# Moving keys ahead of queries, and odd weight pairs into attention's buffers, in a two-layer hybrid decoder trunk

## Chip, cores and metric

The kernel runs on one core of one Trainium2 chip. The metric is device time in microseconds. A core has five engines that work at once, each through its own instructions in order: TensorE (PE, with its weight loads as PEld), VectorE (DVE), ScalarE (ACT), GpSimd (POOL) and SyncE (SP, which here only issues DMAs). Matmuls write PSUM banks; DVE and ACT empty them.

## The reference

Two decoder layers over 512 tokens of width 1024, float32. Each layer normalizes x, projects it, runs two token mixers side by side, adds their gated sum, and then an MLP:

```python
h = rmsnorm(x, norm_mix)
proj = h @ w_in                      # q, k, v of FoX; q, and six k/v of NSA; gates
o_a = fox_attention(...)             # 8 heads, causal softmax with a learned decay
kc, vc = compress_blocks(kc), compress_blocks(vc)      # 31 block summaries
o_c, o_s, o_w = nsa_attention(q_n, kc, vc, ks, vs, kw, vw)   # 8 heads, 2 key/value heads
o_n = g[..., 0:1] * o_c + g[..., 1:2] * o_s + g[..., 2:3] * o_w
mixed = sigmoid(gate_a) * y_a + sigmoid(gate_b) * y_b
x = x + mixed @ w_out
h = rmsnorm(x, norm_mlp)
x = x + square(relu(h @ w_up)) @ w_down                # 1024 -> 4096 -> 1024
```

With 512 tokens the selected branch (s) takes all 8 blocks and the window branch (w) all tokens, so both are plain causal attention with keys ks and kw.

## The kernel before, in words

**Precision and weights.** Every float32 operand is split into a high and a low part (`uh`/`ul`, `wh`/`wl`), and a product is three matmuls: high x high, high x low, low x high (`gemm`, L236 to L238). A weight block is fetched on SP into a raw buffer (`fetch`, L194; tag `raw` has 2 buffers), split by ACT (L210) and DVE (L211), and used. `order` writes out by hand in which order all blocks of both layers are fetched; from the seventh block of the down weights on, they go to one buffer of tag `crs`.

**Who orders the instructions.** The program is written for a framework that gives each instruction the place of its program line as priority, allots buffers by tag as they come free, and orders each engine's queue ahead of the run by a model of the durations. An instruction that is ready early may be placed ahead of earlier lines that are not; on the chip each queue then runs in that order.

**Attention.** `attend` takes units (one head and branch) through three steps: scores, transposes of the softmax, values. Between the steps it draws from a filler generator: 1.8 filler steps per round in FoX, 0.95 in NSA. A projection (`proj`) is 24 matmuls in four filler steps. FoX's filler `fill1` projects the later FoX heads, kc and vc, then runs `compress` in turns with a chain of projections; it ends with the window key kw (block 11 of `wb`). `k_pair` and `q_pair` split the projected rows (ACT, DVE L377) and lay them out for both heads with four DMAs each on SP (L388 into `kk`, L401 into `q`). NSA's filler `fill2` holds `cmp_gen` (`cmp_probs`: the compressed branch of one key/value head, first matmul at L723, which needs two query pairs), `qproj(2)`, `qproj(3)`, and `gated(m)`: two gate projections (DVE multiplies by R at L992), then two output halves. A unit of NSA pair 0 needs query pair 0, ks and kw; its scores are L555 and L558, reduced by DVE at L545. The gate projections and output halves take turns in the two PSUM banks of tag `mm`.

**MLP.** The first 8 of 32 up blocks are plain products. The other 24 make 12 pairs (g = 4 to 15), each a seven-product Strassen scheme (`Strassen.unit`, matmuls at L1382). For a pair, `load` fetches two raw blocks on SP (L1339), adds one half onto another by an accumulating DMA from POOL (L1344, `raw<-raw`), and `third` makes one more sum the same way (L1350 and L1351). `convert` forms two sums on DVE (L1367, L1368) and splits all seven operands (ACT L1371, DVE L1372). Even pairs' raws lie in tag `e` (attention's softmax), odd pairs' in tag `raw`, thirds in `t2`. While pair g is multiplied, pair g + 1 is converted and pair g + 2 loaded. Between the products run down products, whose sums DVE adds to x (L1085), which frees their banks. The activations' sums t3 and t4 lie in tag `va` (4 buffers), which before that held FoX's values and then the mixer's sums MA.

**Constants.** `setup` loads masks and tables (`ct`, L773) and clears `CC`, `kcz` and `vz` on POOL (L781), each with a buffer of its own; the norm's row R lies in tag `r` (L318).

Of the kernel before, what the change touches and what calls it, by code (L numbers as in the profile page):

```python
# [11 lines left out]
F32 = mybir.dt.float32  # L12
# [7 lines left out]
T = 512  # L20
# [123 lines left out]
class Body:  # L144
    def __init__(self, ctx, tc, nc, a):
# [6 lines left out]

    BUFS = dict(raw=2, wh=2, wl=2, uh=8, ul=8, oh=8, ol=8, va=4, t2=12, kd=2, kk=1, zz=4, pt=10, e0=1, ct=1, CC=1, vz=1, q2=3, vn=1, e=2, tmp=3,
                hl=2, r=1, crs=1, small=1, cc=1, s4=6, big=1, kcz=1, g4=2)

# [127 lines left out]

    def rstd(self, acc, tags=("O", "O"), wait=iter(()), exp=True, copy=True):
# [32 lines left out]
        R = self.t("r", [128, T], name="R")[:, :128 * n]  # L317
        nc.scalar.copy(R, ps)  # L318
        return R, rc

# [59 lines left out]
    def k_pair(self, x, fox=None, kd=None):  # L380


        hl = self.hilo(x, 1.0)
        if kd is None:
            kd = self.t("kd", [128, 2, 2, T], F32R)
        for e in range(2):
            for f in range(2):
                self.nc.sync.dma_start(kd[f * 64:(f + 1) * 64, e].bitcast(F32),  # L388
                                         hl[e * 64:(e + 1) * 64].bitcast(F32))
            if fox is not None:  # L390
                h = 2 * fox + e
                self.nc.sync.dma_start(kd[64:66, e, 1].bitcast(F32), self.CC[h:h + 33:32].bitcast(F32))
        return kd
# [22 lines left out]
    def scores(self, u):  # L416
        nc = self.nc
        q, k = u["q"](), u["k"]()
        E = self.t("e", [128, 1280], name="E")
        sm = self.t("s4", [128, NB], name="sm")  # L420
# [111 lines left out]
    def pair_scores(self, u):  # L532
# [3 lines left out]
        q, kk, br, e, other = u["q"](), u["kk"](), u["br"], u["e"], u["other"]  # L536
        E = self.t("e", [128, 1280], name="E")
        if br == 0:
# [10 lines left out]
        for i in range(br, NB):  # L549
            n = 128 * (i + 1)  # L550
            ps = self.p("S")
            qs = q[:, i * 128:(i + 1) * 128]
            for f in range(2):
                if i == 0:
                    nc.tensor.matmul(ps[:, :256].rearrange("p (b c) -> p b c", b=2), qs, kk[:, :, u["hk"], f, :128],  # L555
                                     start=f == 0, stop=f == 1)
                else:
                    nc.tensor.matmul(ps[:, :n], qs, kk[:, br, u["hk"], f, :n], start=f == 0, stop=f == 1)  # L558
# [207 lines left out]
    def setup(self, first):  # L766

        nc, a = self.nc, self.a
        if first:
            self.ident = self.cp.tile([128, 128], F32, name="ident")  # L770
            nc.sync.dma_start(self.ident, a["const"][:, :128])
        self.ct = self.t("ct", [128, 1024])[:, :N_CONST - 128]
        nc.sync.dma_start(self.ct, a["const"][:, 128:])  # L773
        if first:
            self.load_small(0)
        self.mask = self.const("mask")
        self.CC = self.t("CC", [40, T], F32R)
        self.kcz = self.t("kcz", [128, 2, 2, 256], F32R)[:, :, :, :224]
        self.vz = self.t("vz", [128, 2, 2, 128], F32R)
        for t in (self.CC, self.kcz, self.vz):  # L780
            nc.gpsimd.memset(t.bitcast(F32), 0.0)  # L781
# [40 lines left out]
    def order(self, l):  # L822
# [27 lines left out]
    def layer(self, l, u):  # L850
# [8 lines left out]
        for _ in range(6 if l else 8):  # L859
            next(g)  # L860
        self.R, self.rc = R, rc = self.rstd(self.acc, ("O", "O"), wait=g)
        run(g)
# [44 lines left out]
        def fox_unit(h):  # L907
            p, e = divmod(h, 2)
            un = dict(q=lambda: st["qa", p][0][:, e], qx=lambda: st["qa", p][1][e], k=lambda: st["ka", p][:, e], O=[None],
                      ready=lambda: ("qa", p) in st and ("ka", p) in st,  # L910
# [22 lines left out]
        def fill1():  # L933
# [10 lines left out]
        KK = self.t("kk", [128, 2, 2, 2, T], F32R)  # L944
        run(fox_proj(0, ("PT", "PT")))
        self.attend([fox_unit(h) for h in range(8)], fill1(), self.FOX_FILL)


# [3 lines left out]
        def nsa_pair(p):  # L952
# [20 lines left out]
            def unit(br, e):  # L973
                return dict(br=br, e=e, p=p, hk=hk, O=O, after=after, ready=ready[br], kk=lambda: KK,
                            q=lambda: st["qb", p][:, e], v=lambda b: VN[:, b, 2 * br + hk],
# [29 lines left out]
        def fill2():  # L1005
# [58 lines left out]
    def mlp(self, l, x, u, acc, gm):  # L1064
# [50 lines left out]
        for i in range(12):  # L1115
# [149 lines left out]
class Strassen:  # L1265
# [65 lines left out]

    def load(self, g):

        if g < 16:
            b = self.b
            self.raw[g] = []
            for m in (2 * g + 1, 2 * g):
                t = b.t(("e", "raw")[g % 2], [128, 1024], name="raw")
                self.nc.sync.dma_start(t, b.a["wup"][self.l, m].rearrange("p k c -> p (k c)"))  # L1339
                self.raw[g].append(t)  # L1340
            r1, r2 = self.raw[g]
            if g > b.PLAIN // 2:
                self.raw[g].append(self.third(g))
            self.nc.gpsimd.dma_start(r2[:, :512], r2[:, 512:], accum_op=OP.add)  # L1344

    def third(self, g):

        b = self.b
        s3 = b.t("t2", [128, 512], name="s")
        self.nc.sync.dma_start(s3, b.a["wup"][self.l, 2 * g].rearrange("p k c -> p (k c)")[:, :512])  # L1350
        self.nc.gpsimd.dma_start(s3, self.raw[g][0][:, :512], accum_op=OP.add)  # L1351
        return s3

    def convert(self, g):
# [3 lines left out]
        b, nc = self.b, self.nc  # L1358
        if len(self.raw[g]) == 2:
            self.raw[g].append(self.third(g))  # L1360
        r1, r2, s3 = self.raw.pop(g)
# [126 lines left out]
```

## Time and profile before

| what | value |
|---|---|
| median of 3 runs | 1540.74 us (1539.62 to 1543.52) |
| the profiled execution's own time | 1540.51 us |
| its span, first to last instruction | 1538.7 us |
| mean granted TensorE clock | 0.996 |
| busy: PE, DVE, ACT, POOL | 98%, 72%, 53%, 12% |
| moved by DMA | 188.82 MB, 123 GB/s in the mean |

In a profile row, `out<-in` names the tiles written and read, `xN` counts instructions, and a bracket `[1.78 <-DVE gate L992]` gives the engine's idle time before the instruction in us and what ended it. In a view of waits the numbers are the total, the times and the longest. Layer 0 runs from 0 to about 756 us, layer 1 from there on.

### The profile page before, as it was taken

What the parts mean: (1) busy time and instruction counts of PE and PEld (TensorE: products, weight loads), DVE (VectorE), ACT (ScalarE), POOL (GpSimd) and SP (SyncE); (2) the same over time, 40 slices, a digit from 0 to 9 for tenths busy, and PEclk for the clock granted to TensorE, in tenths of its full rate; (3) what the DMA queues carried; (4) which work ended last, traced back from release to release, by engine and by line L of the source; (5) the groups of instructions that cost most, each with busy time, mean ns of one, the idle gap of its engine ahead of it and who ended that gap; (6) DMA issues with size and microseconds to landing.
All of it is one profiled execution on the core that took longest, in us unless ns stands there. A gap on an engine that the chain in (4) does not pass through costs nothing.

```text
span 1538.7 us, 21231 instructions
## 1 busy us (share of the span) xinstructions
PE 1514.2 (98%) x7696; PEld 1264.6 (82%) x7696; DVE 1102.5 (72%) x2124; ACT 811.0 (53%) x1530; POOL 190.1 (12%) x184
## 2 busy tenths in 40 slices
PE   9999999999999999999999999999999999999997
PEld 8878787888888878888888787888888878788897
DVE  5678888777477877775647798877674968777762
ACT  6465555654454655555445555555544636555553
POOL 4000000000201222111310000000002002222122
PEclk9999999999999999999999999999999999999998
DMA  7655322224226555432546542222423365554221
GB/s 261 166 141 150 109 83 84 68 90 162 97 96 177 144 146 140 137 89 87 177 134 179 145 130 83 84 81 69 156 84 97 102 183 135 148 139 136 83 83 55
DMA packets 67576, 188.82 MB, mean 123 GB/s; under 512 B 8560, under 2 KB 9968, under 8 KB 67472
## 3 DMA queue, kind: packets, MB, share of 16 engines
q1 hardware_dynamic: 56672, 168.31, 35.2%
q0 software_dynamic: 6912, 12.59, 5.0%
q10 hardware_dynamic: 3888, 6.58, 1.2%
q8 instruction: 60, 0.98, 0.3%
q14 instruction: 44, 0.36, 0.1%
HBM read 147.53 MB, written 4.19 MB: 99 GB/s over the span
## 4 chain that ended last, share of the span: by engine, by line
PE 83%; DVE 9%; ACT 4%; DMA 3%; issue 2%; SPq 0%; POOL 0%; DVEq 0%; ACTq 0%; POOLq 0%
PE ps_mm L236 11%; PE ps_mm L237 11%; PE ps_mm L238 11%; PE ps_PT L236 3%; PE ps_PT L237 3%; PE ps_PT L238 3%; PE ps_O L1382 3%; PE ps_S L1382 3%; PE ps_mm L1382 2%; PE ps_S L236 2%; PE ps_S L237 2%; PE ps_S L238 2%; PE ps_O L609 2%; PE ps_PT L583 2%; PE ps_O L237 2%; PE ps_O L236 2%
## 5 line engine op out<-in xcount | busy, mean ns | idle before, releaser
L210 ACT CAST wh<-raw 128x1024 fp32r<-128x1024 f32 (+2 forms) x187 | 192.3, 1028 | 261.5 <-issue 81.1
L211 DVE TENSOR_TENSOR wl<-raw,wh 128x1024 fp32r<-128x1024 f32 (+2 forms) x187 | 224.8, 1202 | 48.6 <-ACT wh L210 43.6
L236 PE MATMUL ps_mm<-uh,wh 128*128 128x512 f32 x512 | 204.5, 399 | 0.0
L238 PE MATMUL ps_mm<-uh,wl 128*128 128x512 f32 x512 | 201.8, 394 | 0.0
L237 PE MATMUL ps_mm<-ul,wh 128*128 128x512 f32 x512 | 201.6, 394 | 0.0
L236 PE MATMUL ps_mm<-oh,wh 128*128 128x512 f32 (+1 forms) x316 | 123.4, 392 | 4.0 <-DVE gate L992 3.6
L237 PE MATMUL ps_mm<-ol,wh 128*128 128x512 f32 (+1 forms) x316 | 122.8, 389 | 0.0
L238 PE MATMUL ps_mm<-oh,wl 128*128 128x512 f32 (+1 forms) x316 | 122.6, 388 | 0.0
L238 PEld LDWEIGHTS ps_mm<-uh,wl 128*128 128x128 f32 x512 | 96.4, 188 | 20.8 <-issue 0.8
L236 PEld LDWEIGHTS ps_mm<-uh,wh 128*128 128x128 f32 x512 | 96.4, 188 | 19.3 <-DVE wl L211 1.5
L237 PEld LDWEIGHTS ps_mm<-ul,wh 128*128 128x128 f32 x512 | 96.5, 189 | 16.3
L587 ACT CAST pth<-ps_PT 128x384 fp32r<-128x384 f32 (+1 forms) x96 | 49.1, 513 | 59.0 <-PE ps_PT L583 58.4
L545 DVE CUSTOM_DVE_ANT_0 E<-ps_S,ct 128x384 f32<-128x384 f32 (+3 forms) x112 | 57.1, 514 | 31.1 <-PE ps_S L558 26.8
L1372 DVE TENSOR_TENSOR sl<-raw,sh 128x512 fp32r<-128x512 f32 x96 | 72.7, 760 | 7.2 <-ACT sh L1371 6.4
L546 ACT ACTIVATE E<-E,tiny 128x384 f32<-128x384 f32 (+3 forms) x112 | 65.5, 586 | 21.5 <-DVE tiny L545 21.2
L1371 ACT CAST sh<-raw 128x512 fp32r<-128x512 f32 x96 | 59.1, 617 | 29.4 <-PE ps_mm L1382 10.5
L236 PEld LDWEIGHTS ps_mm<-oh,wh 128*128 128x128 f32 x316 | 59.7, 189 | 17.9 <-DVE gate L992 5.0
L588 DVE TENSOR_TENSOR ptl<-ps_PT,pth 128x384 fp32r<-128x384 f32 (+1 forms) x96 | 57.1, 600 | 18.0 <-ACT pth L587 16.9
L238 PEld LDWEIGHTS ps_mm<-oh,wl 128*128 128x128 f32 x316 | 59.8, 189 | 12.3
L236 PE MATMUL ps_PT<-oh,wh 128*128 128x512 f32 x172 | 67.7, 394 | 2.1 <-DVE x L1085 2.1
L1344 POOL DMA_DIRECT2D raw<-raw x24 | 21.3, 889 | 389.0 <-PE ps_O L609 352.2
L237 PEld LDWEIGHTS ps_mm<-ol,wh 128*128 128x128 f32 x316 | 59.9, 190 | 10.8 <-DVE ol L500 0.4
(444 smaller groups left out, 3989.0 us busy)
## 6 DMA issues: line engine op xcount, KB each, us to landing
raw<-wb SPq DMA_DIRECT2D x64, 512.0 KB, 3.7
raw<-wup SPq DMA_DIRECT2D x64, 512.0 KB, 3.5
raw<-wd SPq DMA_DIRECT2D x48, 512.0 KB, 3.4
w<-w SPq DMA_DIRECT2D x32, 256.0 KB, 4.6
kd<-hl SPq DMA_DIRECT2D x32, 256.0 KB, 5.3
q<-hl SPq DMA_DIRECT2D x64, 128.0 KB, 3.0
raw<-wo SPq DMA_DIRECT2D x16, 512.0 KB, 4.1
raw<-wout SPq DMA_DIRECT2D x16, 512.0 KB, 3.4
```

Of the source, the lines that this page charges most:

```text
L210: nc.scalar.copy(h[:, :n], raw[:, :n])
L211: nc.vector.tensor_tensor(lo[:, :n], raw[:, :n], h[:, :n].bitcast(F32), op=OP.subtract)
L236: mm(ps, h[:, c], xh, start=start and i == 0, stop=False)
L237: mm(ps, h[:, c], xl, start=False, stop=False)
L238: mm(ps, lo[:, c], xh, start=False, stop=stop and i == ks - 1)
L545: nc.vector.tensor_tensor_reduce(e, ps, self.mask[:, T - n:], -1.0, BIG, OP.add, OP.min, mx)
L546: nc.scalar.activation(e, e, AF.Exp, bias=mx, scale=-1.0, accum_out=un["sm"][:, i:i + 1])
L587: nc.scalar.copy(h[:, e, :n], ps[:, :n])
L588: nc.vector.tensor_sub(lo[:, e, :n], ps[:, :n], h[:, e, :n].bitcast(F32))
L1371: nc.scalar.copy(h, src)
L1372: nc.vector.tensor_tensor(lo, src, h.bitcast(F32), op=OP.subtract)
L1382: mm = lambda o, w, x, **kw: self.nc.tensor.matmul(o, w, x, skip_group_check=True, **kw)
```

## The change

In words:

1. In `fill1` kw is projected right after ks, ahead of query pair 0; query pair 1 comes last instead of kw. `order` follows. `KK` is laid out by key/value head, then branch. In `fill2` `gated(4)` runs ahead of `cmp_gen(1)`.
2. Odd pairs' raws and third lie in `va` (three of its four buffers a pair); even pairs' third shares the buffer of the first raw in `e`, now 1536 wide. Pair 4 loads with its third at the head of the MLP, pair 5 right behind it without; its third follows at down product 8 (before, pair 5 loaded at product 10).
3. `ct` with R, and `CC` with `kcz` and `vz`, share two buffers of a new tag `long`, which the MLP uses for t3 and t4. The identity moves into `tiny`.

The diff, without what only passes these along:

```diff
-    BUFS = dict(... va=4, t2=12, kd=2, kk=1, zz=4, pt=10, e0=1, ct=1, CC=1, vz=1, q2=3, vn=1, e=2, ...
+    BUFS = dict(... va=4, t2=12, kd=2, kk=1, zz=4, pt=10, e0=1, long=2, q2=3, vn=1, e=2, ...
...
-            self.ident = self.cp.tile([128, 128], F32, name="ident")
+            self.ident = self.tiny[:, 688:816]
...
-        self.ct = self.t("ct", [128, 1024])[:, :N_CONST - 128]
+        t = self.t("long", [128, 2048], name="ct")
+        self.ct, self.R = t[:, :N_CONST - 128], t[:, 1024:1536]
...
-        self.CC = self.t("CC", [40, T], F32R)
-        self.kcz = self.t("kcz", [128, 2, 2, 256], F32R)[:, :, :, :224]
-        self.vz = self.t("vz", [128, 2, 2, 128], F32R)
+        t = self.t("long", [128, 2048], F32R, name="kcz")
+        self.CC = t[:40, :T]
+        self.kcz = t[:, 512:1408].rearrange("p (h f n) -> p h f n", h=2, f=2)
+        self.vz = t[:, 1408:1920].rearrange("p (h r d) -> p h r d", h=2, r=2)
...
-        for i in (0, 1, 2, 3, 8, 9, 4, 5, 6, 7, 10, 12, 13, 11):
+        for i in (0, 1, 2, 3, 8, 9, 4, 5, 6, 7, 10, 11, 12, 13):
...
-            rest = chain(fox_proj(2), fox_proj(3), proj(10, "ks", lambda ps: self.k_pair(self.roped(ps), kd=KK[:, 0])),
-                         qproj(0), qproj(1))
+            rest = chain(fox_proj(2), fox_proj(3), proj(10, "ks", lambda ps: self.k_pair(self.roped(ps), kd=[t[:, 0] for t in KK])),
+                         proj(11, "kw", lambda ps: self.k_pair(self.roped(ps), kd=[t[:, 1] for t in KK])), qproj(0))
             yield from alternate(c, rest)
-            yield from proj(11, "kw", lambda ps: self.k_pair(self.roped(ps), kd=KK[:, 1]))
+            yield from qproj(1)
...
             yield from qproj(3)
+            yield from gated(4)
             yield from cmp_gen(1)
-            yield from gated(4)
             yield from gated(6)
...
         S.load(g0)
+        S.load(g0 + 1, third=False)
...
-            if i == 10:
-                S.load(g0 + 1)
+            if i == 8:
+                S.third(g0 + 1)
...
-        k34 = [b.t("va", [128, 2, 2, 256], F32R, name="t34") for _ in range(4)]
+        k34 = [b.t("long", [128, 2, 2, 2, 256], F32R, name="t34") for _ in range(2)]
+        k34 = [t[:, i] for t in k34 for i in range(2)]
...
-    def load(self, g):
+    def load(self, g, third=True):
...
-            for m in (2 * g + 1, 2 * g):
-                t = b.t(("e", "raw")[g % 2], [128, 1024], name="raw")
+            if g % 2:
+                r1, r2, s3 = (b.t("va", [128, 1024], name="raw") for _ in range(3))
+                self.raw[g] = [r1, r2, s3[:, :512]]
+            else:
+                r1, r2 = (b.t("e", [128, 1536], name="raw") for _ in range(2))
+                self.raw[g] = [r1[:, :1024], r2[:, :1024], r1[:, 1024:]]
+            for m, t in zip((2 * g + 1, 2 * g), self.raw[g]):
                 self.nc.sync.dma_start(t, b.a["wup"][self.l, m].rearrange("p k c -> p (k c)"))
-                self.raw[g].append(t)
-            r1, r2 = self.raw[g]
-            if g > b.PLAIN // 2:
-                self.raw[g].append(self.third(g))
+            r1, r2, _ = self.raw[g]
+            if third:
+                self.third(g)
             self.nc.gpsimd.dma_start(r2[:, :512], r2[:, 512:], accum_op=OP.add)
...
-        s3 = b.t("t2", [128, 512], name="s")
+        s3 = self.raw[g][2]
```

More of the change, by code (lines that the diff above doesn't have):

```diff
@@ L151, in __init__ @@
         self.dp = P("dp", 1, space=bass.MemoryType.DRAM)
-    BUFS = dict(raw=2, wh=2, wl=2, uh=8, ul=8, oh=8, ol=8, va=4, t2=12, kd=2, kk=1, zz=4, pt=10, e0=1, ct=1, CC=1, vz=1, q2=3, vn=1, e=2, tmp=3,
-                hl=2, r=1, crs=1, small=1, cc=1, s4=6, big=1, kcz=1, g4=2)
+    BUFS = dict(raw=2, wh=2, wl=2, uh=8, ul=8, oh=8, ol=8, va=4, t2=12, kd=2, kk=1, zz=4, pt=10, e0=1, long=2, q2=3, vn=1, e=2, tmp=3,
+                hl=2, r=1, crs=1, small=1, cc=1, s4=6, big=1, g4=2)
     TINY = dict(s4=(4, 12), sm=(4, 8), g4=(4, 2), s16=(16, 2), s32=(32, 5), z=(32, 1), th=(96, 1), gates=(96, 1))
@@ L282, in table, with rstd @@
         self.nc.scalar.activation(self.t("s4", [128, 1], name="warm"), after[:, :1], f)
-    def rstd(self, acc, tags=("O", "O"), wait=iter(()), exp=True, copy=True):
+    def rstd(self, acc, tags=("O", "O"), wait=iter(()), exp=True, copy=True, R=None):
         nc = self.nc
@@ L316, in rstd @@
             return rows(tags[2]), R
-        R = self.t("r", [128, T], name="R")[:, :128 * n]
+        if R is None:
+            R = self.t("r", [128, T], name="R")[:, :128 * n]
         nc.scalar.copy(R, ps)
@@ L384, in k_pair @@
         if kd is None:
-            kd = self.t("kd", [128, 2, 2, T], F32R)
+            t = self.t("kd", [128, 2, 2, T], F32R)
+            kd = [t[:, 0], t[:, 1]]
         for e in range(2):
             for f in range(2):
-                self.nc.sync.dma_start(kd[f * 64:(f + 1) * 64, e].bitcast(F32),
+                self.nc.sync.dma_start(kd[e][f * 64:(f + 1) * 64].bitcast(F32),
                                          hl[e * 64:(e + 1) * 64].bitcast(F32))
@@ L391, in k_pair @@
                 h = 2 * fox + e
-                self.nc.sync.dma_start(kd[64:66, e, 1].bitcast(F32), self.CC[h:h + 33:32].bitcast(F32))
+                self.nc.sync.dma_start(kd[e][64:66, 1].bitcast(F32), self.CC[h:h + 33:32].bitcast(F32))
         return kd
@@ L418, in scores @@
         q, k = u["q"](), u["k"]()
-        E = self.t("e", [128, 1280], name="E")
+        E = self.t("e", [128, 1536], name="E")
         sm = self.t("s4", [128, NB], name="sm")
@@ L536, in pair_scores @@
         q, kk, br, e, other = u["q"](), u["kk"](), u["br"], u["e"], u["other"]
-        E = self.t("e", [128, 1280], name="E")
+        E = self.t("e", [128, 1536], name="E")
         if br == 0:
@@ L554, in pair_scores @@
                 if i == 0:
-                    nc.tensor.matmul(ps[:, :256].rearrange("p (b c) -> p b c", b=2), qs, kk[:, :, u["hk"], f, :128],
+                    nc.tensor.matmul(ps[:, :256].rearrange("p (b c) -> p b c", b=2), qs, kk[:, :, f, :128],
                                      start=f == 0, stop=f == 1)
                 else:
-                    nc.tensor.matmul(ps[:, :n], qs, kk[:, br, u["hk"], f, :n], start=f == 0, stop=f == 1)
+                    nc.tensor.matmul(ps[:, :n], qs, kk[:, br, f, :n], start=f == 0, stop=f == 1)
             if i == 0:
@@ L860, in layer @@
             next(g)
-        self.R, self.rc = R, rc = self.rstd(self.acc, ("O", "O"), wait=g)
+        R, rc = self.rstd(self.acc, ("O", "O"), wait=g, R=self.R)
         run(g)
@@ L908, in fox_unit @@
             p, e = divmod(h, 2)
-            un = dict(q=lambda: st["qa", p][0][:, e], qx=lambda: st["qa", p][1][e], k=lambda: st["ka", p][:, e], O=[None],
+            un = dict(q=lambda: st["qa", p][0][:, e], qx=lambda: st["qa", p][1][e], k=lambda: st["ka", p][e], O=[None],
                       ready=lambda: ("qa", p) in st and ("ka", p) in st,
@@ L937, in fill1 @@
             c = self.compress(st["kc"], st["vc"], small, l)
-            rest = chain(fox_proj(2), fox_proj(3), proj(10, "ks", lambda ps: self.k_pair(self.roped(ps), kd=KK[:, 0])),
-                         qproj(0), qproj(1))
+            rest = chain(fox_proj(2), fox_proj(3), proj(10, "ks", lambda ps: self.k_pair(self.roped(ps), kd=[t[:, 0] for t in KK])),
+                         proj(11, "kw", lambda ps: self.k_pair(self.roped(ps), kd=[t[:, 1] for t in KK])), qproj(0))
             yield from alternate(c, rest)
-            yield from proj(11, "kw", lambda ps: self.k_pair(self.roped(ps), kd=KK[:, 1]))
+            yield from qproj(1)
         self.pc = {}
         KK = self.t("kk", [128, 2, 2, 2, T], F32R)
+        KK = [KK[:, 0], KK[:, 1]]
         run(fox_proj(0, ("PT", "PT")))
@@ L973, in unit @@
             def unit(br, e):
-                return dict(br=br, e=e, p=p, hk=hk, O=O, after=after, ready=ready[br], kk=lambda: KK,
+                return dict(br=br, e=e, p=p, hk=hk, O=O, after=after, ready=ready[br], kk=lambda: KK[hk],
                             q=lambda: st["qb", p][:, e], v=lambda b: VN[:, b, 2 * br + hk],
@@ L1348, in third @@
         b = self.b
-        s3 = b.t("t2", [128, 512], name="s")
+        s3 = self.raw[g][2]
         self.nc.sync.dma_start(s3, b.a["wup"][self.l, 2 * g].rearrange("p k c -> p (k c)")[:, :512])
         self.nc.gpsimd.dma_start(s3, self.raw[g][0][:, :512], accum_op=OP.add)
-        return s3
     def convert(self, g):
@@ L1358, in convert @@
         b, nc = self.b, self.nc
-        if len(self.raw[g]) == 2:
-            self.raw[g].append(self.third(g))
         r1, r2, s3 = self.raw.pop(g)
```

1 line of the change is left out of this document (removed).

## The prediction, made before the changed kernel was run

> **What bounds the kernel now.** First the page: its span, the busy times and the chain by engine.
>
> ```profile
> span 1538.7 us, 21231 instructions
> PE 1514.2 (98%) x7696; PEld 1264.6 (82%) x7696; DVE 1102.5 (72%) x2124; ACT 811.0 (53%) x1530; POOL 190.1 (12%) x184
> PE 83%; DVE 9%; ACT 4%; DMA 3%; issue 2%; SPq 0%; POOL 0%; DVEq 0%; ACTq 0%; POOLq 0%
> ```
>
> TensorE is the bound; the change neither adds nor removes a matmul. So only the 1538.7 - 1514.2 = 24.5 us in which PE idles can move, and stretches where it runs slowly. The view of windows says where those are (columns: window, length, then busy us and count of PE, PEld, DVE, ACT, POOL, then the granted clock, DMA share, GB/s).
>
> ```profile
> 173.00:196.00 23.00, 20.16 (x103) 15.05 (x102) 19.50 (x58) 15.96 (x41) 0.00 (x0) 1.00 0.19 59
> 929.00:952.00 23.00, 20.20 (x94) 15.02 (x93) 17.79 (x54) 14.28 (x35) 0.00 (x0) 0.93 0.20 59
> 510.00:556.00 46.00, 44.08 (x228) 36.56 (x227) 37.50 (x48) 29.18 (x52) 14.44 (x12) 1.00 0.57 155
> 560.00:700.00 140.00, 139.77 (x698) 117.12 (x697) 103.36 (x134) 78.24 (x132) 29.02 (x26) 1.00 0.44 122
> 1256.00:1315.00 59.00, 54.84 (x280) 45.42 (x280) 43.16 (x60) 34.23 (x60) 14.36 (x12) 1.00 0.51 141
> ```
>
> The first two are the start of NSA attention in layers 0 and 1: PE idles 23.00 - 20.16 = 2.84 and 23.00 - 20.20 = 2.80 us. 510:556 and 1256:1315 are the first Strassen units of the two MLPs: 1.92 and 4.16 us. The later units (560:700) lose 0.23 us in 140. The view of waits over the whole span names what PE stood for at NSA:
>
> ```profile
> PE ps_mm L236 <- DVE gate L992: 3.6, 2, 1.8
> PE ps_S L723 <- DMA q<-hl: 1.3, 2, 1.0
> PE ps_PT L583 <- DVE ptl L588: 1.2, 2, 0.6
> ```
>
> L723 (cmp_probs) waits for a query pair, in the midst of NSA, 1.3 us in all. So 2.84 + 2.80 + 1.92 + 4.16 + 1.3 = 13.0 us of idle time lie at places that the change touches.
>
> **Part 1: keys ahead of queries.** Now pair 0's scores need kw, projected last. Timelines of PE, DVE and SP at layer 0:
>
> ```profile
> 174.05 0.48 PE L555 MATMUL ps_S<-kk,q 128*128 128x256 f32 x2 [0.23 <-DMA kk<-hl]
> 175.30 2.02 PE L723 MATMUL ps_S<-q,kcz 128*128 128x512 f32 x8
> 182.87 0.50 PE L236 MATMUL ps_mm<-oh,wh 128*128 128x512 f32 x1 [1.78 <-DVE gate L992]
> 161.47 0.74 DVE L361 STREAM_SHUFFLE tmp<-ps_mm 128x512 f32<-128x512 f32 x1
> 174.57 0.29 DVE L545 CUSTOM_DVE_ANT_0 E<-ps_S,ct 128x128 f32<-128x128 f32 x1 [1.95 <-PE ps_S L555]
> 182.13 0.69 DVE L992 TENSOR_TENSOR gate<-ps_mm,R 128x512 f32<-128x512 f32 x1
> 930.62 0.29 DVE L545 CUSTOM_DVE_ANT_0 E<-ps_S,ct 128x128 f32<-128x128 f32 x1 [1.87 <-PE ps_S L555]
> 167.27 1.81 SPq L388 DMA_DIRECT2D kk<-hl  x3
> 172.60 0.46 SPq L388 DMA_DIRECT2D kk<-hl  x1
> ```
>
> kw's projection left PSUM at 161.47; its copies were issued from 167.27, the fourth only at 172.60 behind a weight load, and the first scores ran at 174.05. Until then PE worked ahead on gate projections, so it barely waited (0.23), but VectorE had no scores to reduce and idled 1.95 us. It paid later: its backlog put the gate's product, which frees PE's bank, at 182.13, and PE stood 1.78. With kw two projections earlier (KK in place before the last query projection) the scores can start as soon as PSUM has room, and the 1.95 us (1.87 in layer 1) are used. The gate would end at 182.13 + 0.69 - 1.95 = 180.87, before PE is ready for it at 182.87 - 1.78 = 181.09. I take the whole gate wait, **-3.6**, and the key wait, **-0.2**; bounds 0 and the idle time itself, 5.6. I leave the 1.2 us at L583, since VectorE stays the late one there. The other moves of this part are free: as many projections, copies and DMAs are issued as before, kw's four copies trade places with query pair 1's four on SP, and the rearranged KK has the same size per instruction.
>
> In layer 1 the same gap has a second price. PE after it, and the window's clock:
>
> ```profile
> 938.97 0.74 PE L236 MATMUL ps_mm<-oh,wh 128*128 128x512 f32 x1 [1.83 <-DVE gate L992]
> 939.00:942.40 3.40, 3.40 (x8) 2.75 (x9) 3.40 (x11) 1.01 (x3) 0.00 (x0) 0.51 0.00 0
> ```
>
> For 3.40 us the clock was 0.51, right behind the 1.83 us gap: about 3.40 x 0.49 = 1.7 us lost while PE counts as busy. If the gap goes, I take that too, **-1.7**. Layer 0's gap of 1.78 us left the clock at 1.00, so it isn't sure. The Trainium skill, "TensorE: Matmul & The Clock Gate", section "HAM oscillation — how this bites in real kernels", asks only that PE have no idle gap over some 3.4 us. By that rule a gap of 1.83 us would not be the cause and the term would be 0; the row (half clock directly behind the gap) speaks against it, layer 0 for it.
>
> **The wait that part 1 adds.** Query pair 1 is now the last projection, and cmp_gen(0), the first filler of NSA, multiplies it at L723. Behind L723 on PE, in order, stand all scores and projections. The same nearness existed for cmp_gen(1), right behind qproj(3), and cost 1.3 us in the two layers. I take **+1.3**; lower end 0 (at 175.30 L723 didn't wait), upper end the slower rival below.
>
> **Part 2: gated(4) ahead of cmp_gen(1).** Twelve fill steps (two projections, two output halves) now lie between qproj(3) and its use. VectorE, SP and PE there, and a window of plain products:
>
> ```profile
> 236.08 0.74 DVE L361 STREAM_SHUFFLE tmp<-ps_mm 128x512 f32<-128x512 f32 x1
> 241.62 2.67 SPq L401 DMA_DIRECT2D q<-hl  x4
> 247.32 0.71 PE L723 MATMUL ps_S<-q,kcz 128*128 128x512 f32 x2 [1.00 <-DMA q<-hl]
> 355.00:377.00 22.00, 22.00 (x101) 18.03 (x100) 17.04 (x25) 8.80 (x13) 0.67 (x2) 1.00 0.37 108
> ```
>
> From PSUM to the landed copies it took 247.32 - 236.08 = 11.2 us. gated(4) is two projections of 24 matmuls and two halves of 12, 72 x 22.00/101 = 15.7 us of PE, and the attention's own steps lie between, so the wait goes: **-1.3**, between 0 and that. Pair 2's second branch needs cmp_gen(1) only later.
>
> **Part 3: odd pairs of raw weights in va, early.** VectorE's groups at L1367 (the sum s2, which reads the accumulated raw) in the first units of layers 0 and 1, then layer 1 on SP and VectorE, and PE's wait there:
>
> ```profile
> L1367 DVE TENSOR_TENSOR s<-raw 128x512 f32<-128x512 f32 x5 | 3.8, 762 | 12.0 <-DMA raw<-raw 9.3 <-issue 2.6
> L1367 DVE TENSOR_TENSOR s<-raw 128x512 f32<-128x512 f32 x5 | 3.6, 726 | 14.3 <-DMA raw<-raw 14.3
> 1239.51 8.12 SPq L1339 DMA_DIRECT2D raw<-wup  x4
> 1259.48 0.69 DVE L1367 TENSOR_TENSOR s<-raw 128x512 f32<-128x512 f32 x1 [7.07 <-DMA raw<-raw]
> 1298.85 0.69 DVE L1367 TENSOR_TENSOR s<-raw 128x512 f32<-128x512 f32 x1 [3.36 <-DMA raw<-raw]
> PE ps_PT L236 <- DVE x L1085: 2.1, 1, 2.1
> ```
>
> Pairs 6 and 5 were fetched together only at 1239.51, since pair 5 shared the two raw buffers with the down weights. VectorE blocked 7.07 us on its accumulation, and behind that the sums L1085 that free PE's banks came late: 2.1 us. With va, which the mixer frees before w_out, pair 5 is loaded before w_out instead, and this wait goes: **-2.1**. Pair 7 finds the fourth va buffer free, pair 9 one left by pair 5. Even pairs stay in two buffers and cannot be earlier: pair 8 (at 1298.85) can still hold VectorE 3.36 us. The rest of PE's idle time in these two windows is 1.92 in layer 0 and 4.16 - 2.1 = 2.06 in layer 1. It follows pairs of both kinds, so I take half, **-2.0**; ends 0 and -4.0. VectorE waits 12.0 us at L1367 in layer 0 and PE idles only 1.92 there, which is why I don't take more.
>
> The moved loads, five per layer ahead of w_out (pair 4's third, pair 5's three, one of pair 7; 2 x 256 + 3 x 512 KB = 2.1 MB), come between the end of NSA and w_out's first products:
>
> ```profile
> 341.00:355.00 14.00, 14.00 (x73) 11.71 (x72) 8.39 (x16) 5.83 (x10) 0.88 (x2) 1.00 0.92 324
> raw<-wout SPq DMA_DIRECT2D x16, 512.0 KB, 3.4
> 364.12 10.76 SPq L194 DMA_DIRECT2D raw<-wout  x3
> 390.39 1.83 POOL L277 TENSOR_TENSOR acc<-sq 128x512 f32<-128x512 f32 x1 [34.72 <-ACT sq L267]
> ```
>
> From 355 to 377 the DMA engines are 0.37 busy; at the 324 GB/s of the window before, 2.1 MB take 6.5 us. w_out's first load is issued at 364.12; POOL's first norm sum, two blocks of 24 matmuls (5.2 us each) after its first product, is at 390.39, so that product is near 380. Those 15 us cover a landing of 3.4, the 6.5 and the conversion. Without that cover a layer would pay at most the 6.5. Their accumulations on POOL stand ahead of its norm sums, behind a wait of 34.72 us. Cost 0.
>
> **Part 4: constants share long.** The SP issues of the constants, a memset and their first reader in layer 1:
>
> ```profile
> L773 SPq DMA_DIRECT2D ct<-const x2: 400/415/430, 13.1 to 341.7; - x2
> L781 POOL MEMSET kcz<- x2: 842/848/854, 1.2 to 249.7; 128x896 f32 x2
> 713.88 0.39 PE L1382 MATMUL ps_S<-b,sh 128*128 128x512 f32 x1
> 810.39 0.39 PE L806 MATMUL ps_S<-ct,tiny 128*8 128x128 f32 x2 [0.29 <-DVE tiny L799]
> ```
>
> Layer 1's constants loaded at 341.7 and were cleared on POOL at 249.7; now both wait for t34's last product, about when the last Strassen unit ends (713.88), 96 us before the first use at 810.39. R's new place changes no duration. Cost 0; were that cover gone, a landing of some 4 us.
>
> **The sum**: -3.6 - 0.2 - 1.7 + 1.3 - 1.3 - 2.1 - 2.0 = **-9.6 us**. The profiled execution took 1540.51 (span 1538.7 and 1.8 around it), 0.2 below the median of 1540.74: **1530.9**.
>
> **Rivals.**
> - *All goes*: every idle us counted above and the slow clock (13.0 + 1.7 = 14.7) vanish and L723 doesn't wait: 1525.8. For it: VectorE is 72% busy and has room. Against: the L583 waits and the even pairs aren't touched. Chance 0.12.
> - *The half clock isn't the gap's*: it falls somewhere else in the span, so its 1.7 us stay: 1532.6. Layer 0's gap without it speaks for this. It is what the page named above would make of it. Chance 0.15.
> - *Waits only change places* (the change doesn't do what it says): VectorE's backlog at NSA comes from its own work (19.50 of 23 us busy), so the gate is as late as before, and even pairs keep blocking it; only pair 5's 2.1 us go, and part 1's new wait eats part 2's gain: 1538.4. Chance 0.16.
> - *Slower: L723 reaches query pair 1 too early.* With scores ready at once, PE may run them and cmp_gen(0) where it now does gate projections. Pair 1 lands 161.47 + 11.2 = 172.7 by part 2's interval; L723 follows the first scores by 175.30 - 174.05 = 1.25 us, so at worst it stands from 162.7, 10 us in each layer. Then 1540.5 - 10.9 + 20 = 1549.6. It decides from 5.4 us a layer, that is L723 reached before 167.3. For it: PE keeps its order. Against: now single gate matmuls stand between those of FoX's last heads, so the order is made with such waits in view. Chance 0.12.
>
> The forecast keeps 0.45. A measurement of this kernel can tell about 0.3% (4.6 us) from no change. Faster: 0.45 + 0.12 + 0.15, less 0.02 for a forecast that comes out small, 0.70; within 0.3%: 0.16 + 0.02, 0.18; slower 0.12. Range 1525.5 to 1541: it takes in the bounds of the terms, all cases but the slower one, and so some 0.85.
>
> **What the profile of the changed kernel would show.** Part 1: no wait of PE on kk, VectorE's first NSA reduction without its 1.9 us gap, the gate wait gone, the clock 1.00 there; L723 is the row of the added wait. Part 2: no q wait at the second L723. Part 3: pair 5's loads before w_out's, L1367's idle time well under 12.0 and 14.3, PE's idle time in the first units under 1.92 and 4.16. I am wrong if the gate wait is still there, if L723 waits more than 1 us a layer, or if w_out's or layer 1's first products wait for a load.

## The result and the profile after

| kernel | median us | runs (lowest to highest) |
|---|---|---|
| before | 1542.61 | 15 (1539.62 to 1544.32) |
| after | 1537.02 | 15 (1534.34 to 1541.67) |

The ratio is 0.9969, 95% interval 0.996 to 0.9978: 4.8 us faster (3.4 to 6.2), half of the forecast 9.6. The new median lies in the range (1525.5 to 1541), 6 us above the predicted 1530.9.

From the page of the kernel after, its span and the busy times:

```profile
span 1533.7 us, 21178 instructions
PE 1508.6 (98%) x7696; PEld 1263.3 (82%) x7696; DVE 1098.6 (72%) x2124; ACT 812.6 (53%) x1530; POOL 190.5 (12%) x184
```

The span is 5.0 us shorter, yet PE's idle time is not: 1533.7 - 1508.6 = 25.1 us, against 24.5. So idle time was taken away in one place and came back in another, and the saving stands in PE's busy time (1514.2 -> 1508.6). The prediction had said that only idle time and stretches at a low clock can move; the mean clock went from 0.996 to 0.997, some 1.5 us by estimate, which is not all of the 5.6. The windows of the kernel after (columns as in the prediction; 510:556 and 1256:1315 are some us further into the MLPs than before):

```profile
0.00:20.00 20.00, 16.10 (x69) 13.24 (x70) 7.24 (x11) 10.74 (x16) 10.04 (x18) 1.00 0.74 242
173.00:196.00 23.00, 21.79 (x115) 17.78 (x114) 22.17 (x59) 15.72 (x38) 0.00 (x0) 1.00 0.20 69
929.00:952.00 23.00, 21.85 (x114) 17.48 (x112) 21.80 (x61) 15.53 (x36) 0.00 (x0) 1.00 0.18 56
510.00:556.00 46.00, 43.03 (x224) 36.00 (x223) 37.96 (x50) 28.23 (x51) 12.80 (x11) 1.00 0.49 134
1256.00:1315.00 59.00, 54.33 (x272) 45.48 (x272) 40.52 (x55) 33.84 (x59) 13.87 (x12) 0.97 0.49 135
```

And the first 20 us of the kernel before:

```profile
0.00:20.00 20.00, 18.90 (x79) 15.94 (x80) 9.70 (x12) 12.41 (x19) 10.89 (x19) 1.00 0.79 264
```

- NSA's starts: idle 2.84 -> 1.21 and 2.80 -> 1.15 us, 12 and 20 more matmuls in the same 23 us, the clock 1.00 in both. Nearly as predicted: the gate wait is gone, but a shorter one, of 1.2 us in each layer (L560 in the view below), stands there now.
- The first Strassen units: idle 1.92 -> 2.97 and 4.16 -> 4.67 us, and the clock 0.97 in layer 1. The prediction had them fall by 4.1.
- The start: idle 1.10 -> 3.90. The prediction had nothing here.

The view of waits of the kernel after names the new ones (the Strassen matmul L1382 is now L1389, the sums for x L1085 are L1090, s2's L1367 is L1374; the experiments shift by a few lines again):

```profile
PE ps_mm L1389 <- DVE x L1090: 4.1, 1, 4.1
PE ps_S L350 <- ACT uh L258: 2.7, 1, 2.7
PE ps_S L560 <- DVE tiny L547: 2.4, 2, 1.2
PE ps_S L1389 <- ACT y L1413: 2.0, 2, 1.9
```

The gate, the keys and the query pairs are gone from it, and so is the 2.1 us behind pair 5. In their place stand one wait in layer 1's MLP, longer than any before, one in layer 0's, one at the start, and the 1.2 us (L560) in each NSA start. The timeline around the first of them (pair 9):

```profile
1281.95 9.28 SPq L1350 DMA_DIRECT2D raw<-wup  x2
1295.01 0.89 POOL L1354 DMA_DIRECT2D raw<-raw  x1 [6.24 <-DVE z L1447]
1300.49 0.69 DVE L1374 TENSOR_TENSOR s<-raw 128x512 f32<-128x512 f32 x1 [3.68 <-DMA raw<-raw]
1302.23 0.68 DVE L1436 TENSOR_TENSOR y<-y,ps_S 128x512 f32<-128x512 f32 x1
1304.03 0.68 DVE L1090 TENSOR_TENSOR x<-x,ps_PT 128x512 f32<-128x512 f32 x1
1304.77 0.50 PE L1389 MATMUL ps_mm<-t,sh 128*128 128x512 f32 x1 [4.11 <-DVE x L1090]
```

Read it from the top. The second issue of the first row ends at 1281.95 + 9.28 = 1291.23: that is pair 9's second raw. POOL starts its accumulation at 1295.01, and it lands at 1300.49, 5.5 us later. VectorE stands at s2 for 3.68 us, though it has other work: y and the sum for x stand behind s2 in its queue, and PE's next product starts right as that sum ends (1304.03 + 0.68), after 4.11 us. Whole span, s2 before and after (total idle time ahead of it in the last column):

```profile
L1367 DVE TENSOR_TENSOR s<-raw 128x512 f32<-128x512 f32 x24 | 27.2, 1133 | 30.8 <-DMA raw<-raw 27.8 <-issue 2.6
```
```profile
L1374 DVE TENSOR_TENSOR s<-raw 128x512 f32<-128x512 f32 x24 | 20.6, 857 | 19.6 <-DMA raw<-raw 19.5
```

The early loads did their part: VectorE stands at s2 a third less. But the place of pair 9's s2 changed. To see it apart from the earlier start of the whole MLP, here is VectorE in order_only, an experiment below that has the new order and the old buffers:

```profile
1300.24 0.67 DVE L1087 TENSOR_TENSOR x<-x,ps_PT 128x512 f32<-128x512 f32 x1
1304.08 0.69 DVE L1369 TENSOR_TENSOR s<-raw 128x512 f32<-128x512 f32 x1 [3.16 <-DMA raw<-raw]
```

There s2 stands behind the sum for x and waits nearly as long, while PE lost 1.2 us at that sum. In the kernel after, s2 runs 3.6 us earlier, ahead of y and of the sum. Less waiting in all, at a worse place.

### The profile page after: what moved, and what is told of

Read it like the earlier page. It is cut to its first block, busy times and chain, and to the rows that moved or that the text cites. A ratio compares the mean times of both kernels' runs of the same rounds, so it can differ in the third digit from the quotient of the medians.

```text
span 1533.7 us, 21178 instructions
## 1 busy us (share of the span) xinstructions
PE 1508.6 (98%) x7696; PEld 1263.3 (82%) x7696; DVE 1098.6 (72%) x2124; ACT 812.6 (53%) x1530; POOL 190.5 (12%) x184
## 4 chain that ended last, share of the span: by engine, by line
PE 89%; DVE 5%; ACT 2%; DMA 2%; issue 1%; POOL 0%; SPq 0%; DVEq 0%; POOLq 0%; ACTq 0%
PE ps_mm L236 12%; PE ps_mm L238 12%; PE ps_mm L237 12%; PE ps_PT L236 3%; PE ps_PT L237 3%; PE ps_PT L238 3%; PE ps_O L1389 3%; PE ps_S L1389 3%; PE ps_mm L1389 3%; PE ps_O L611 2%; PE ps_PT L585 2%; PE ps_S L236 2%; PE ps_S L237 2%; PE ps_S L238 2%; PE ps_PT L1389 2%; PE ps_O L236 2%
## 5 line engine op out<-in xcount | busy, mean ns | idle before, releaser
L1379 DVE TENSOR_TENSOR sl<-raw,sh 128x512 fp32r<-128x512 f32 x120 | 91.0, 766 | 25.2 <-ACT sh L1378 24.2
L1378 ACT CAST sh<-raw 128x512 fp32r<-128x512 f32 x120 | 73.0, 618 | 6.8 <-PE ps_O L1389 2.7
L238 PE MATMUL ps_PT<-oh,wl 128*128 128x512 f32 x172 | 67.3, 391 | 0.0
```

Source lines behind the costliest of these rows:

```text
L238: mm(ps, lo[:, c], xh, start=False, stop=stop and i == ks - 1)
L1378: nc.scalar.copy(h, src)
L1379: nc.vector.tensor_tensor(lo, src, h.bitcast(F32), op=OP.subtract)
```

## Experiments

Theory A: the order (parts 1 and 2) gave the predicted gain or more, and the buffers (parts 3 and 4) took part of it back. The place is the second raw of a pair: it is loaded last, into the buffer that comes free last, and needs an accumulation after that, and s2 blocks VectorE for it. Rival B: the order gave only the 5 us and the buffers nothing, or what the MLP loses has another cause than that chain, such as the moved traffic. All ratios are to the kernel before on the same chip; us are the ratio by its median there (1542.33, 1542.19 and 1542.76 in the three groups).

| kernel | order | buffers, constants | second raw | median us | ratio, 95% |
|---|---|---|---|---|---|
| order_only | both | before's | last | 1530.7 | 0.9926 [0.9912, 0.994] |
| buffers_only | before's | after's | last | 1547.59 | 1.0035 [1.0024, 1.0047] |
| after_r2 | both | after's | first | 1525.65 | 0.9892 [0.9876, 0.9908] |
| order_const | both | constants of after | last | 1534.28 | 0.9948 [0.993, 0.9966] |
| fill1_only | part 1 | before's | last | 1535.07 | 0.9953 [0.9941, 0.9965] |
| fill2_only | part 2 | before's | last | 1541.45 | 0.9996 [0.9986, 1.0006] |
| order_r2 | both | before's | first | 1529.42 | 0.9923 [0.9907, 0.994] |
| after_r2_late | both | after's, set up later | first | 1525.45 | 0.9891 [0.9879, 0.9904] |
| order_r2_b | both | before's | first | 1526.74 | 0.9893 [0.9879, 0.9908] |
| after_r2_b | both | after's | first | 1525.38 | 0.9889 [0.9873, 0.9905] |
| after_load | both | after's | loaded first | 1525.55 | 0.9885 [0.9868, 0.9901] |
| order_r2ct | both | constants of after | first | 1528.65 | 0.9908 [0.9893, 0.9922] |

**The order alone, and the rest alone.** order_only is the kernel before with the diff's lines of `order`, `fill1`, `fill2` and `KK`; buffers_only is the kernel after with the first three undone.

> The kernel before with the new order alone: window key right after the selected key, query pair 1 last, gated(4) ahead of cmp_gen(1), KK by head. Raw buffers and constants as before. Theory (the order gave all of the gain and the buffers gave part of it back): PE's idle time at the two NSA starts falls from 2.84 and 2.80 us to about 1.2 each, no q wait at the second cmp_probs, no half clock there, MLP as before: 9 to 11 us below before. Rival (buffers and order share the gain): 5 us or less below before.

> The changed kernel with the order of projections, gated and cmp_gen as before: early odd raws in va, constants in long, identity in tiny. Theory: no gain, the first Strassen units and the start lose what they lose in the changed kernel, so 2 to 5 us above before. Rival (early loads do help, and what the changed kernel loses comes from the mix with the new order): 3 to 5 us below before.

-11.4 us (9.3 to 13.6) and +5.4 us (3.7 to 7.2), each a little beyond what was expected: together about -6, the change's -4.8 within the intervals. Rival B's first half falls. Waits of order_only, then of buffers_only:

```profile
PE ps_PT L236 <- DVE x L1087: 2.7, 1, 2.7
PE ps_S L559 <- DVE tiny L546: 2.2, 2, 1.1
```
```profile
PE ps_mm L1389 <- DVE x L1090: 4.0, 1, 4.0
PE ps_mm L236 <- DVE gate L997: 3.6, 2, 1.8
PE ps_S L1389 <- ACT y L1413: 2.5, 2, 2.4
PE ps_S L725 <- DMA q<-hl: 2.1, 2, 1.1
```

The gate and query waits go with the order; the MLP's long waits (4.0 and 2.4) come with the buffers. In order_only PE idles 1.08 and 1.09 us in the windows of the two NSA starts.

**Parts 1 and 2 by themselves.**

> Kernel before with part 1 alone (kw projected ahead of the query pairs, KK in two halves). By the prediction's terms, without the added wait that the kernel after didn't show, this is -3.6 - 0.2 - 1.7 = -5.5 us against the kernel before: both gate waits and the half clock at the start of NSA gone, PE's loss at NSA's start under 3 us in both layers, and the two waits of the compressed scores on a query pair (1.3 us) still there. By the rival, that part 2's move is what relieves VectorE there, part 1 alone gives under 3 us and the loss stays above 4 us in a layer.

> Kernel before with part 2 alone (gated(4) ahead of cmp_gen(1)). By the prediction's term -1.3 us: the wait of the compressed scores on the query pair is gone, the gate waits (3.6) and the key wait stay. By the rival it carries what part 1 doesn't explain of the 11.4 us that both gave together, 5 us or more.

-7.2 us (5.4 to 9.1) and -0.6 (-2.2 to +0.9). fill1_only's waits have no gate and still the two query waits; fill2_only's the reverse:

```profile
PE ps_S L559 <- DVE tiny L546: 2.2, 2, 1.1
PE ps_S L724 <- DMA q<-hl: 1.4, 2, 0.8
```
```profile
PE ps_mm L236 <- DVE gate L992: 3.6, 2, 1.8
```

So each part removes its own wait, and part 1 carries most; part 2's gain can't be told from none. Their sum, -7.8, is less than the -11.4 of both; the intervals (4.5 to 11.3 added, 9.3 to 13.6) overlap, and whether the two help one another stays open.

**The second raw first.** after_r2 changes nothing but the order within `load`; after_load keeps its first half only.

```diff
-            for m, t in zip((2 * g + 1, 2 * g), self.raw[g]):
-                self.nc.sync.dma_start(t, ...)
             r1, r2, _ = self.raw[g]
+            for m, t in ((2 * g, r2), (2 * g + 1, r1)):
+                self.nc.sync.dma_start(t, ...)
+            self.nc.gpsimd.dma_start(r2[:, :512], r2[:, 512:], accum_op=OP.add)   # not in after_load
             if third:
                 self.third(g)
-            self.nc.gpsimd.dma_start(r2[:, :512], r2[:, 512:], accum_op=OP.add)   # kept in after_load
```

> The changed kernel, with the second raw block of every pair (the one that is accumulated onto itself) loaded into the first buffer that comes free, the first block into the next. Theory A (VectorE is held at s2 because the block with the longer chain, load and accumulation, gets the later buffer): VectorE's idle time at L1374 falls from 19.6 us to under 8, PE's waits of 4.1 and 1.9 us in the first Strassen units go, 4 to 6 us below the changed kernel. Theory B (s2 is put into VectorE's queue as early as its data is modelled to be there, and stands there for as long as the accumulation takes beyond that): the waits of about 3 us stay and only move forward, no gain beyond 1 us.

> The kernel after with the second raw loaded first and accumulated ahead of the third, once more, beside the others on one chip: 1525.3 to 1526.2 as before, with runs close together, since no gap of PE over 2 us is left for the clock to follow.

> The kernel after with only the load order changed: the second raw is loaded first, but on POOL's queue the third's accumulation still stands ahead of the second raw's. If the load is the late end of the chain, most of the 11 us that the two edits give together comes: 1526 to 1529, s2's idle time 4 to 8 us. If POOL's queue is (the third's accumulation waits for the first raw, which now comes last), the time is 1533 to 1537 and s2 waits 15 us or more.

1525.65, 1525.38 and 1525.55 us: some 17 us under the kernel before (0.9885 to 0.9892) and 11 to 12 under the kernel after, about twice what was expected of the swap. s2's group in after_r2 and in after_load:

```profile
L1374 DVE TENSOR_TENSOR s<-raw 128x512 f32<-128x512 f32 x24 | 16.4, 685 | 4.3 <-DMA raw<-raw 3.7 <-DMA raw<-wup 0.6
```
```profile
L1374 DVE TENSOR_TENSOR s<-raw 128x512 f32<-128x512 f32 x24 | 16.4, 685 | 5.4 <-DMA raw<-raw 4.6 <-DMA raw<-wup 0.7
```

The starts of the two MLPs as windows, in the kernel after and in after_r2:

```profile
470.00:565.00 95.00, 92.03 (x453) 76.95 (x452) 73.99 (x100) 48.89 (x82) 17.48 (x16) 1.00 0.52 147
1225.00:1330.00 105.00, 100.33 (x487) 83.68 (x487) 75.47 (x104) 52.75 (x89) 19.96 (x18) 0.98 0.49 138
```
```profile
470.00:565.00 95.00, 94.47 (x466) 78.97 (x465) 76.91 (x104) 49.89 (x84) 19.09 (x17) 1.00 0.54 150
1225.00:1330.00 105.00, 104.00 (x515) 86.89 (x515) 80.35 (x107) 55.51 (x94) 21.93 (x19) 1.00 0.53 148
```

PE's idle time falls from 2.97 to 0.53 and from 4.67 to 1.00 us, 6.1 us in all. PE also gets through 13 and 28 more matmuls in these windows; at 0.20 us each (105 us / 515) that is, by estimate, 8 of the 11 to 12 us. The DMA share rises a little, so traffic is not the cause, and rival B falls whole. after_load tells which half counts: the load. Pair 8 in after_load (the second of the two issues in the first row is its second raw):

```profile
1262.95 8.40 SPq L1351 DMA_DIRECT2D raw<-wup  x2
1275.30 0.91 POOL L1354 DMA_DIRECT2D raw<-raw  x1 [5.47 <-DVE wl L211]
1282.10 0.68 DVE L1374 TENSOR_TENSOR s<-raw 128x512 f32<-128x512 f32 x1
```

The same pair in the kernel after, where the second raw is the one issued at 1281.95 (above):

```profile
1273.50 0.33 SPq L1350 DMA_DIRECT2D raw<-wup  x1
1286.19 0.91 POOL L1354 DMA_DIRECT2D raw<-raw  x1 [0.66 <-DVE sl L1379]
1289.58 0.69 DVE L1374 TENSOR_TENSOR s<-raw 128x512 f32<-128x512 f32 x1 [2.90 <-DMA raw<-raw]
```

There the two loads lie 8.5 us apart, the second raw comes last, and s2 waits 2.90 us. In after_load the second raw has the buffer that comes free first; its accumulation starts at 1275.30, and s2 follows without a wait. Which issue belongs to which pair is read from the accumulation that starts some 4 us after it.

**Second raw first, with before's buffers.** order_r2, and order_r2_b beside after_r2_b:

> Both moves of the order and before's buffers, but the second raw of each pair is loaded ahead of the first, and accumulated ahead of the third. By the theory that the chain of load and accumulation (some 8 us, and 4 more when the second raw has the buffer that comes free last) is what holds VectorE in the first Strassen units: VectorE's idle time at s2 falls from about 31 us in both layers to under 15, PE's loss at the two MLP starts from 3.4 and 8.6 to about 2 and 4, and the time is 4 to 7 us under the 1530.7 of the kernel with the order alone. By the rival, that the early loads into va are needed for it, s2 waits as before and the time is 1530 to 1531.

> Both moves of the order and before's buffers, second raw first: once more, on one chip with the kernel after in that form. By the theory that the chain of load and accumulation is the main cause: under 1529 and PE's loss at the two MLP starts near 3.2 and 3.8 us as in the first profile; 2 to 4 us behind the kernel after with the second raw first, whose s2 waits 4.3 us in all instead of 14.3. By the rival that the gain needs the early loads: 1530 to 1531, as with the order alone.

It is one kernel, measured twice: 1529.42 with runs from 1525.75 to 1535.87, then 1526.74 (1526.0 to 1527.15). In order_r2_b, s2's group and the two windows:

```profile
L1369 DVE TENSOR_TENSOR s<-raw 128x512 f32<-128x512 f32 x24 | 16.4, 684 | 15.1 <-DMA raw<-raw 13.8 <-DMA raw<-wup 1.2
```
```profile
470.00:565.00 95.00, 93.29 (x459) 77.73 (x458) 75.22 (x103) 49.41 (x83) 20.54 (x19) 1.00 0.61 166
1225.00:1330.00 105.00, 103.82 (x512) 86.13 (x511) 78.58 (x105) 55.94 (x94) 23.01 (x21) 1.00 0.58 158
```

Two swapped loads in the old buffers halve s2's wait (31.2 us in order_only), and PE's idle time in these windows is 1.71 and 1.18 us, against 1.49 and 4.71 in order_only. In time the two measurements differ: by their ratios the swap gives 0.5 us over order_only (0.9923 against 0.9926) or 5 us (0.9893). By the second, on one chip with after_r2_b, the new buffers add only 1.4 us (1526.74 - 1525.38), where 2 to 4 were expected. How much of after_r2's gain the old buffers keep stays open.

**The constants.** order_const adds part 4 to order_only, order_r2ct to order_r2_b. after_r2_late is after_r2 with layer 0's `setup` at weight chunk 3 instead of 1.

> The new order with the constants and t34 in long, R and the identity moved, raws as before. It tells the 2.7 us that PE waits for ScalarE's split of x at 17 us in the changed kernel: if the constants' new place makes it, this run has it too and is 2 to 3 us above order_only; if the raw buffers make it, this run is within 1 us of order_only. MLP as before in both.

> Both moves of the order, the second raw first, and part 4 (constants with t34 in the shared tile), raw buffers as before: no early loads into va. Against order_r2_b it is part 4 alone: 2 to 4 us slower if the constants' tile costs the start as between order_only and order_const (3.6). Against after_r2_b it is part 3 alone: 4 to 8 us slower if the early loads and va are worth the s2 waits of 14 against 4 us plus the start, 0 to 2 if they are not.

> The kernel after with the second raw first, and layer 0's constants set up two weight chunks later, so that all loads of x stand ahead of them on SP. By the theory that the constants' larger shared tile takes the room of two x tiles at the start, and the last x loads wait for the first squares: no wait of PE on uh at 20 us (1.3 in the kernel with the second raw first), PE's loss in the first 20 us 3.0 to 3.4 instead of 4.1, and 0.5 to 1.5 us less than 1525.65. By the rival, that the start's loss is the weights' or the clock's, the loss and the time stay within 0.3 us.

Part 4 costs 3.6 us (1534.28 - 1530.7) and 1.9 us (1528.65 - 1526.74). Against after_r2_b, order_r2ct lacks part 3 alone: part 3 is worth 3.3 us once the second raw is loaded first, between the two expectations. Waits of order_const:

```profile
PE ps_PT L236 <- DVE x L1090: 2.3, 1, 2.3
PE ps_S L350 <- ACT uh L258: 2.0, 1, 2.0
```

The wait for uh at the start is there, as expected if the constants make it, and the 4 us wait in layer 1's MLP is not: that one belongs to part 3. The intervals of such neighbours overlap (each is some 2 us either way); the two pairs agree in sign. SP's start in the kernel before, in the kernel after and in after_r2_late:

```profile
8.23 1.28 SPq L1229 DMA_DIRECT2D x<-xT  x3
14.41 0.80 SPq L1229 DMA_DIRECT2D x<-xT  x2
```
```profile
8.65 0.43 SPq L776 DMA_DIRECT2D ct<-const  x1
15.09 3.34 SPq L1235 DMA_DIRECT2D x<-xT  x4
```
```profile
8.27 1.76 SPq L1235 DMA_DIRECT2D x<-xT  x4
```

In the kernel after, four loads of x stand behind the constants and the first squares, and PE waits 2.7 us for uh at 20 us. With `setup` later all go ahead and that wait is gone (idle time in the first 20 us 1.10 again), but PE waits 0.9 us for a split weight (L351 on wl) at 37 us instead, and the time falls by 0.2 us only. The rival was right about the time: the x loads are not what part 4 costs by themselves. The windows say where most of it sits: in the first 150 us PE idles 1.84 us in order_only and 6.07 in order_const, 2.23 in order_r2_b and 5.70 in order_r2ct. The late setup lowers it from 4.33 (after_r2) to 3.32, with 2.22 of that now after the first 20 us, against 0.72 there in the kernel before. So most of part 4's cost lies at the start, in more waits than the one for uh; what makes the others wasn't tested.

## Why the prediction came out as it did

- **Part 1** (-3.6 -0.2 -1.7): right, and too small. The gate wait, the key wait and the half clock at 939 are gone, and part 1 alone gave -7.2. The timeline of the kernel after has the first scores at 166.60 instead of 174.05, and VectorE's first reduction without the gap of 1.95 us:

```profile
166.60 0.40 PE L557 MATMUL ps_S<-kk,q 128*128 128x256 f32 x2
167.53 0.29 DVE L547 CUSTOM_DVE_ANT_0 E<-ps_S,ct 128x128 f32<-128x128 f32 x1
```

What I summed was the idle time of waits. The counts say more: 12 and 20 more matmuls in the windows of the two NSA starts, at 0.20 us each (23 us / 115), are by estimate 6.4 us, while the idle time that went is 3.3 us and the half clock 1.7. A stop costs PE more than its idle time: in the trace of the kernel before, gate matmuls in a row start 0.23 us apart, but each record lasts 0.39, so 0.16 us behind a stop count as busy. For two stops that is 0.3 us, so it is not all of the difference; the rest stays open.
- **The added wait** (+1.3): did not come. In the kernel after, the compressed scores ran from 171.9 to 174.9 with nothing that PE waited for. The slower rival, with this wait grown to 10 us a layer, has nothing for it.

```profile
L725 PE MATMUL ps_S<-q,kcz x8: 390/394/398, 171.9 to 174.9; 128*128 128x512 f32 x8
```

- **Part 2** (-1.3): the wait is gone as predicted; alone it measured -0.6 (-2.2 to +0.9), an interval that holds both -1.3 and 0.
- **Part 3** (-2.1 -2.0): this step failed. The early loads came as predicted (pair 5's at 1120.23 and 1127.60, ahead of the MLP), nothing late in w_out came of it, s2's total wait fell, and the 2.1 us behind pair 5 went. What failed is the -2.0, half of the rest taken as gain, and with it the sum of the part: the two MLP starts lost 1.6 us more (1.92 + 4.16 -> 2.97 + 4.67), not 4.1 less. I had written of pair 8 that it "can still hold VectorE 3.36 us" (it held 2.90) and counted on idle time falling with s2's wait. I did not ask what moves when a wait in the middle of an in-order queue goes: s2 of pair 9 went 3.6 us forward against order_only, to ahead of the sums that it had stood behind, and still before its data, so that PE stood 4.11 us behind it. Pair 9's first raw could come early, but s2 needs the second. buffers_only has this wait too (4.0), order_const, without part 3, does not. What part 3 costs by itself is less sure, and its sign hangs on the load order: order_const to after, on different chips and both against before, is 0.9948 to 0.9969, some 3 us slower with part 3 (the intervals just overlap); with the second raw first it is 3.3 us faster.
- **Part 4** (0): failed, +1.9 to +3.6. I looked at the constants' readers and at layer 1, not at what else SP issues at the start; the first 150 us carry most of the cost.
- **The rivals**: "waits only change places" gave 1538.4, nearest to the measured 1537.0, but by a mechanism that did not happen (gate unchanged, new wait at L723). That its time is near is luck. The places that changed were the MLP's and the start. *The half clock isn't the gap's* is open: the half clock at 939 went, but the kernel after has one at 1305.50, and the same gate gap stood without it elsewhere (last section). So the forecast's time failed through parts 3 and 4: about -11.4 from the order, where I had -5.5, and +6.6 (0.9926 to 0.9969) from the rest, where I had -4.1.
- **Not shown**: why VectorE's queue has s2 that early. The order is made ahead from modelled durations; a model that has the accumulation land sooner than 5.5 us would do it. That is argued from the queue's order only.

## What to carry to other kernels

When a wait inside an in-order queue is relieved, look at what stands behind the instruction that moves: idle time of a helper engine may fall while the bound engine waits longer. In a chain of load and accumulation, issue first the load that has work after it, above all when buffers come free one by one: here two swapped loads were worth some 11 us in the new buffers, more than the whole change, and between 0.5 and 5 us in the old ones. Constants that move to other buffers can cost where they are loaded, far from their readers (1.9 to 3.6 us here).

## What the runs showed of the hardware

**Half clock behind some gaps, whatever their length.** Windows directly behind a gap of PE: in the kernel after behind 4.11 us, and behind 2.71 us at the start; in after_r2_b behind 2.19 us at the start:

```profile
1305.50:1308.80 3.30, 3.30 (x12) 2.81 (x11) 1.80 (x2) 2.56 (x5) 1.28 (x1) 0.50 0.00 0
19.75:23.05 3.30, 3.30 (x14) 2.74 (x15) 2.91 (x3) 3.30 (x6) 1.95 (x2) 1.00 0.97 313
```
```profile
19.40:22.70 3.30, 3.30 (x8) 2.62 (x9) 2.92 (x3) 3.30 (x6) 1.96 (x2) 0.50 1.00 338
```

A half clock of some 3.3 us costs some 1.6 us beside the gap. But in these traces the length of the gap does not decide. A lower clock stood behind 1.78 us (fill2_only, 182.97: 0.68 over 3.30 us), 1.83 us (before, 938.97), 2.67 us (order_only, 1249.65: 0.53 over 3.25 us) and 2.75 us (fill2_only, 1259.71: 0.54); it stayed 1.00 behind 1.78 us (before, 182.87), 1.83 us (fill2_only, 939.60), 2.12 us (before, 1260.91), 2.31 us (order_const, 1257.17) and 2.71 us. Of the six gate gaps of before, fill2_only and buffers_only, all of 1.78 to 1.83 us, two had it. So the prediction's -1.7 stood on a half clock that the same gap brings in one execution and not in another; what decides stays open. The Trainium skill, "TensorE: Matmul & The Clock Gate", section "HAM oscillation — how this bites in real kernels", asks only that PE have no idle gap over some 3.4 us; here the half clock came behind shorter gaps too.

Gaps and clock may also explain the scatter: the kernel before ran from 1537.33 to 1546.34 on one chip; after_r2, with no wait over 1.3 us in its profile, from 1525.29 to 1525.76. The expectation that after_r2_b, the same kernel, has no gap over 2 us failed: its profiled run is the one of 1528.68, with 2.19 us and the half clock shown above. One such run does not prove it.

**s2 itself got faster** with the second raw first: 1133 ns in the mean in the kernel before, 685 in after_r2 and 684 in order_r2_b. The traces show when it was slow. In the kernel before, 14 of the 24 ran beside POOL's subtraction L1450 (`ol<-y,oh`), took 0.84 to 1.78 us and ended some 0.55 us after it; the other 10 ran alone and took 0.68 or 0.69. In order_r2_b none ran beside that subtraction, and all took 0.68 or 0.69, beside POOL's DMA issues too. The Trainium skill, "SBUF — State Buffer", "SBUF: two separate sides", says that a VectorE operation with two SBUF inputs and a GpSimd operation that reads SBUF lock each other out; these rows agree, though no run changed this alone.
